# Reordering the column tiles of a projection so that each head pair's three tiles stand together

## The chip, the core and the metric

The kernel runs on one core of a Trainium2 chip. The time is the device time of one execution in microseconds (us). The engines are TensorE (PE; PEld is its weight loads), VectorE (DVE), ScalarE (ACT), GpSimd (POOL) and SyncE (SP), whose queue issues the DMAs here. Each engine works through its own queue in order; semaphores set by the other engines release what waits.

## What is computed

One layer of a mixed model over T = 2048 tokens of width 1024. The normalized input is multiplied by `w_in` (1024 x 3712, here 29 column tiles of 128), and the columns go to three branches, whose results go through one output projection:

```
h = rms_norm(x, pre_norm_g[i])
z = h @ w_in[i]
...
out_a = spatial_gating(u_a, v_a, ...) * silu(g_a)
out_b = conv_module(val_b, glu_b, ...) * silu(g_b)
out_c = rwkv7_mix(z[..., oc:og], ...) * silu(z[..., og:])
mix = concatenate([out_a, out_b, out_c]) @ w_out[i]
```

The third branch is a recurrence with eight heads of 64, worked on in four pairs. For each pair it needs a tile each of r, k and v. Ahead of the recurrence come a token shift, the decay (a small two-stage product with a sigmoid), the normalization of k within each head (`kk * rsqrt(max(sum(kk*kk), 1e-12))`) and the sum of r·k·r_k within each head, which multiplies v.

## The kernel before

The tokens are projected in two halves of 1024 (half 0 and half 1). A column tile of a half is `gemm` (L295 to L303): 48 matmuls of 128x512, three products of high and low parts in fp32r, eight steps of the inner dimension, two groups of tokens. Its result stands in one of two PSUM buffers `z` (`zps`), so that a tile can begin only when what reads the tile two places ahead of it is done. Half 0 projects all 29 tiles; half 1 projects the first 23 in this loop, and the last six (10, 11, 25 to 28) are spread out in `tail()`, beside the recurrence. Half 0 also splits each weight tile into parts (ScalarE L282, GpSimd L283) and stores them; half 1 reloads them.

The order of the tiles is the list `ORDER` (L349). `TG` gives each tile's place in it. The steps that use a tile are generators that yield due times made from `TG`; the scheduler takes these as priorities and sets each engine's order when the program is built. Nothing else is written out by hand for the projection.

What hangs on the tiles:

- Head pair p has the tiles 12+p (r), 16+p (k) and 20+p (v). `s_prep` prepares it: the small products of the decay (TensorE L469, L474; ScalarE L476, L478), a scan (VectorE L481), the token shift of each tile (ScalarE L329; VectorE L330, and L333 in half 1), the square of k (ScalarE L496), its high and low parts (`parts`: ScalarE L231, GpSimd or VectorE L232), the sums within heads on TensorE (`sums`, L240), the maximum (VectorE L501), the square root (ScalarE L503), four reciprocals (`recip`, VectorE L245), L505. After the v tile: VectorE L515 and L517; GpSimd L521, ScalarE L522, GpSimd L523; VectorE L525 and GpSimd L526; eight transposes of v (TensorE L537) with their copies (ScalarE L539); the product r·k (VectorE L546), its parts (L231, L232), the sums (TensorE L240), and L553 and L554.
- Tiles 4 and 5 need one ScalarE instruction (L592). Tiles 0 and 1 need a VectorE product (L595), small matmuls (TensorE L603) and two more VectorE steps (L607, L610).
- Tiles 8, 6, 9 and 7 feed a convolution over 31 taps: VectorE L452, 120 instructions over both halves. `s_pw` (L613) normalizes its result: sums (L240 with `onesm`), VectorE L625, ScalarE L630, sums again, ScalarE L637, the same `recip` (VectorE L245), VectorE L641, ScalarE L642.
- The recurrence begins, after the projection of half 1, with score matmuls at L819 and VectorE L824.

In the rows z, m and c are PSUM tiles, w weight tiles, h the normalized input, and L, mk, pg and inv work tiles.

Of the kernel before, what the change touches and what calls it, by code (L numbers as in the profile page):

```python
# [34 lines left out]
def hybrid_kernel(ctx, tc, x, x_t, w_in, vecs, wup, pw_w, sgu_wt, sgu_lnb, sgu_b,  # L35
# [310 lines left out]

    ORDER = [2, 8, 3, 6, 24, 9, 7, 12, 16, 13, 20, 17, 21, 4, 14, 0, 18, 22, 15, 19, 5, 23, 1, 10, 11, 25, 26, 27, 28]  # L349
    NG = len(ORDER)  # L350
    NT = 6
    LORD = [2, 3] + [ct for ct in ORDER if ct not in (2, 3)]
    TG = {ct: i for i, ct in enumerate(ORDER)}
    W, Z, H, X = {}, {}, {}, {}
# [38 lines left out]
    def s_gemm():  # L393
        for half in range(2):
# [5 lines left out]
            while n < (NG if half == 0 else NG - NT):  # L400
                two = half == 0 and n == NG - 2
                yield b0 + n
                cts = ORDER[n:n + 2] if two else ORDER[n:n + 1]
                for ct in cts:
# [282 lines left out]
    def tail():  # L687

        cts = ORDER[NG - NT:]
        for n, ct in enumerate(cts[:-2]):  # L690
# [655 lines left out]
```

## Time and profile before

| | before |
|---|---|
| three runs | 1484.35, 1481.45, 1483.39 us |
| median | 1483.39 us |
| the profiled execution | 1479.78 us |
| its span, first to last instruction | 1477.8 us |
| mean granted clock of TensorE | 0.977 |
| TensorE busy | 1389.8 us (94%) |
| VectorE busy | 997.8 us (68%) |
| ScalarE busy | 575.1 us (39%) |
| GpSimd busy | 351.4 us (24%) |

The busy shares are means over the whole span. Half 0 is projected from about 80 us to 430 us, half 1 from there to about 720 us, and the recurrence follows. In a timeline row, the first number is the start in us from the beginning of the span, the second the time from the first instruction's start to the last one's end, x the number of instructions; the bracket is the idle time ahead of it and what released it.

### The profile page before, as it was taken

The page shows a single profiled execution, that of the slowest core. Times are in us where ns is not written, and L with a number is a line of the kernel's source. Part 1 is how long each engine was busy: PE and PEld are TensorE (multiplying, and loading weights), DVE is VectorE, ACT ScalarE, POOL GpSimd, SP SyncE. Part 2 cuts the span into 40 slices and gives each one's busy share as a digit, 9 for nine tenths or more (in the row PEclk, how much of TensorE's full clock was granted, in tenths as well). Part 3 has the DMA queues.
Part 4 walks back from the last instruction along what each step waited for, and adds up shares of the span by engine and source line. Part 5 has one row for each costly group of instructions (what it writes and reads, how often), then busy time and mean ns, then how long its engine had stood idle before and what let it go on. Part 6 is the DMA issues. An engine that isn't in the chain of part 4 may idle for free.

```text
span 1477.8 us, 24438 instructions
## 1 busy us (share of the span) xinstructions
PE 1389.8 (94%) x9701; PEld 1108.8 (75%) x9701; DVE 997.8 (68%) x1963; ACT 575.1 (39%) x900; POOL 351.4 (24%) x324
## 2 busy tenths in 40 slices
PE   7999999999999999899898888989888999999998
PEld 6876777786798787678676767767766777888887
DVE  6599993674537999567767587687687654555553
ACT  6343344556322344454433444534434443212121
POOL 5443454542401023133211211211212100111110
PEclk9999999999999999999999999999999999999999
DMA  8432466579435457646724732233231443323231
GB/s 325 154 132 87 133 200 202 182 260 317 174 112 168 169 179 211 208 138 190 233 86 174 227 115 88 73 116 100 73 113 61 144 132 128 133 103 129 101 131 43
DMA packets 158311, 223.29 MB, mean 151 GB/s; under 512 B 58236, under 2 KB 108149, under 8 KB 158198
## 3 DMA queue, kind: packets, MB, share of 16 engines
q1 hardware_dynamic: 158066, 221.68, 45.6%
q8 instruction: 76, 1.25, 0.4%
q14 instruction: 37, 0.30, 0.1%
q10 hardware_dynamic: 132, 0.06, 0.0%
HBM read 132.58 MB, written 89.13 MB: 150 GB/s over the span
## 4 chain that ended last, share of the span: by engine, by line
PE 65%; DVE 24%; ACT 4%; issue 3%; DMA 2%; POOL 1%; DVEq 0%; ACTq 0%; POOLq 0%; SPq 0%
PE z L300 27%; PE z L1160 12%; PE z L1047 8%; DVE inv L452 7%; PE c L1137 3%; DVE inv L872 3%; PE z L312 2%; DVE inv L877 2%; PE m L819 2%; DVE mk L245 2%; PE m L240 1%; DVE L L975 1%; PE m L1116 1%; POOL L L268 1%; PE c L960 1%
## 5 line engine op out<-in xcount | busy, mean ns | idle before, releaser
L300 PE MATMUL z<-h,w 128*128 128x512 f32 x2592 | 636.1, 400 | 7.0 <-ACT zl L336 3.3
L300 PEld LDWEIGHTS z<-h,w 128*128 128x128 f32 x2592 | 486.8, 190 | 128.0 <-issue 7.1
L1047 PE MATMUL z<-h,w 128*128 128x512 f32 x768 | 211.4, 420 | 0.7 <-DVE w L1034 0.7
L452 DVE SCALAR_TENSOR_TENSOR inv<-inv,vc,inv 128x1024 f32<-128x1024 f32 x120 | 191.0, 1610 | 1.6
L1047 PEld LDWEIGHTS z<-h,w 128*128 128x128 f32 x768 | 143.8, 197 | 32.5 <-DVE w L1034 1.1
L283 POOL TENSOR_TENSOR w<-w,w 128x1024 fp32r<-128x1024 f32 x26 | 74.2, 2853 | 123.0 <-PE z L300 95.5
L1160 PE MATMUL z<-L,w 128*128 128x512 f32 (+1 forms) x384 | 96.4, 394 | 0.0
L1160 PE MATMUL z<-h,w 128*128 128x512 f32 (+1 forms) x384 | 93.3, 391 | 0.8 <-DVE inv L1143 0.8
L1144 ACT ACTIVATE inv<-inv 128x512 f32<-128x512 f32 (+1 forms) x33 | 20.4, 619 | 182.3 <-DVE inv L1143 182.3
L872 DVE TENSOR_TENSOR inv<-inv,inv 128x48 f32<-128x48 f32 (+23 forms) x464 | 87.5, 222 | 2.4
L1104 POOL TENSOR_TENSOR inv<-inv,pg 128x1024 f32<-128x1024 f32 x16 | 38.3, 2395 | 208.6 <-DMA inv<-mx_s 122.7
L877 DVE TENSOR_TENSOR inv<-inv,inv 128x48 f32<-128x48 f32 (+23 forms) x464 | 84.3, 218 | 1.2
L1160 PEld LDWEIGHTS z<-h,w 128*128 128x128 f32 x384 | 71.3, 188 | 17.3 <-DVE inv L1143 1.2
L1143 DVE TENSOR_TENSOR inv<-z,L 128x512 f32<-128x512 f32 (+1 forms) x32 | 21.9, 683 | 89.7 <-PE z L1160 89.7
L1160 PEld LDWEIGHTS z<-L,w 128*128 128x128 f32 x384 | 70.5, 188 | 15.5
L977 POOL TENSOR_TENSOR ri<-ri,pc 128x256 f32<-128x256 f32 x31 | 21.5, 695 | 240.3 <-DVE L L975 162.5
L245 DVE RECIPROCAL mk<-mk 128x256 f32<-128x256 f32 x40 | 65.8, 1709 | 18.1 <-ACT mk L503 9.3
L824 DVE TENSOR_TENSOR mk<-m,mask 128x512 f32<-128x512 f32 x58 | 37.6, 686 | 45.9 <-PE m L819 41.4
L819 PE MATMUL m<-L,L 64*128 64x128 f32 x464 | 44.9, 303 | 17.6 <-DVE inv L872 15.2
L828 ACT COPY inv<-mk 32x128 f32<-32x128 f32 x128 | 37.9, 296 | 55.3 <-DVE mk L824 52.4
L819 PEld LDWEIGHTS m<-L,L 64*128 64x128 f32 x464 | 37.2, 201 | 24.8 <-issue 20.0
L312 PE MATMUL z<-w,h 128*128 128x256 f32 x384 | 52.7, 293 | 0.9 <-ACT h L262 0.9
(246 smaller groups left out, 2019.9 us busy)
## 6 DMA issues: line engine op xcount, KB each, us to landing
w_s<-w SPq DMA_DIRECT2D x58, 512.0 KB, 3.3
w<-w_s SPq DMA_DIRECT2D x58, 512.0 KB, 5.2
w<-in_w_in_dram SPq DMA_DIRECT2D x26, 512.0 KB, 3.7
L<-in_x_dram SPq DMA_DIRECT2D x16, 512.0 KB, 7.9
ar_s<-L SPq DMA_DIRECT2D x16, 512.0 KB, 5.4
wo_s<-w SPq DMA_DIRECT2D x16, 512.0 KB, 3.4
L<-ar_s SPq DMA_DIRECT2D x32, 256.0 KB, 3.2
L<-bk_s SPq DMA_DIRECT2D x32, 256.0 KB, 4.1
```

The lines of the kernel that those rows point to most:

```text
L245: nc.vector.reciprocal(t[:, g * 256:(g + 1) * 256], t[:, g * 256:(g + 1) * 256])
L283: nc.gpsimd.tensor_tensor(out=ws[1], in0=wr, in1=ws[0], op=ALU.subtract)
L300: nc.tensor.matmul(z[:, g * 512:(g + 1) * 512], lhsT=ws[a][:, k * 128:(k + 1) * 128], rhs=h[:, b, k, :], start=(n == 0), stop=(n == 23))
L312: nc.tensor.matmul(z[:, i * 256:(i + 1) * 256], lhsT=h[:, b, k, i * 128:(i + 1) * 128], rhs=ws[k // 4][a][:, (k % 4) * 256:(k % 4 + 1) * 2 ...
L452: nc.vector.scalar_tensor_tensor(out=ac, in0=y[:, i:i + HT], scalar=col(V_CW + 2 * i + ct), in1=ac, op0=ALU.mult, op1=ALU.add)
L819: nc.tensor.matmul(sp[par][:, p, :], lhsT=bk[lo:lo + 64, p, :], rhs=ar[lo:lo + 64, p, :], start=True, stop=True)
L872: nc.vector.tensor_tensor(out=tmp[:, o:o + n, :m], in0=tl[:, lo:hi, m:m + 1].to_broadcast([128, n, m]), in1=ml[:, m, :m].unsqueeze(1).to_b ...
L877: nc.vector.tensor_tensor(out=tl[:, lo:hi, :m], in0=tl[:, lo:hi, :m], in1=tmp[:, o:o + n, :m], op=ALU.add)
L1047: nc.tensor.matmul(mx[:, nh * 512:(nh + 1) * 512], lhsT=oT[a][:, k, :], rhs=wo[k // 4][:, b, k % 4, nh * 512:(nh + 1) * 512], start=(k == ...
L1104: nc.gpsimd.tensor_tensor(out=x2, in0=x2, in1=pg[0], op=ALU.mult)
L1137: nc.tensor.matmul(pp, lhsT=pT[:, a, k, :], rhs=gw[8 + k][b][:, nh * 512:(nh + 1) * 512], start=(n == 0), stop=(n == 5))
L1160: nc.tensor.matmul(z, lhsT=xT[a][:, k, :], rhs=gw[k][b][:, sl], start=(k == 0 and n == 0), stop=(k == 7 and n == 2))
```

## The change

Only the list `ORDER` is changed.

```diff
-    ORDER = [2, 8, 3, 6, 24, 9, 7, 12, 16, 13, 20, 17, 21, 4, 14, 0, 18, 22, 15, 19, 5, 23, 1, 10, 11, 25, 26, 27, 28]
+    ORDER = [2, 8, 3, 6, 24, 9, 7, 12, 16, 20, 4, 0, 13, 17, 21, 5, 14, 18, 22, 1, 15, 19, 23, 10, 11, 25, 26, 27, 28]
```

The first nine tiles stay, and so do the last six. Between them, each pair's r, k and v now stand in a row. Pair 0 (12, 16, 20) is followed by 4 and 0, pair 1 (13, 17, 21) by 5, pair 2 (14, 18, 22) by 1, and pair 3 (15, 19, 23) by tile 10. The order holds for both halves.

In the order of TensorE's instructions, half 0, the sum of pair 0's r·k (m_1356 and m_1360, L240 on `ones64`) stands in z_1569, the product of tile 14:

```order
L300 MATMUL z_1569<-h_224,w_1346 128x512
L300 MATMUL z_1569<-h_224,w_1345 128x512 x2
L300 MATMUL z_1569<-h_224,w_1346 128x512
L240 MATMUL m_1356<-mk_1352,ones_83 128x512
L300 MATMUL z_1569<-h_224,w_1345 128x512
L240 MATMUL m_1360<-mk_1352,ones_83 128x512
L300 MATMUL z_1569<-h_224,w_1345 128x512
```

Now that sum (m_1245 and m_1249) stands in z_1367, the product of tile 13:

```order
L300 MATMUL z_1367<-h_289,w_1139 128x512
L300 MATMUL z_1367<-h_289,w_1138 128x512
L240 MATMUL m_1245<-mk_1241,ones_83 128x512
L240 MATMUL m_1249<-mk_1241,ones_83 128x512
L300 MATMUL z_1367<-h_289,w_1138 128x512
L469 MATMUL c_1321<-mk_766,ri_122 128x512
L474 MATMUL c_1321<-mk_766,yc_123 128x512
```

It has moved two tiles ahead, and short matmuls of pair 1 (L469, L474) stand just behind it.

VectorE's order at the same place, from pair 0's L515 to its L546, before:

```order
L515 SCALAR_TENSOR_TENSOR L_1234<-mk_1048,L_896 128x8x64
L515 SCALAR_TENSOR_TENSOR L_1238<-mk_1048,L_896 128x8x64
L517 TENSOR_TENSOR L_1238<-L_979,L_896 128x8x64
L452 SCALAR_TENSOR_TENSOR inv_894<-inv_890,vc,inv_894 128x1024 x2
L525 TENSOR_TENSOR mk_1048<-mk_1048,L_916 128x1024
L452 SCALAR_TENSOR_TENSOR inv_894<-inv_890,vc,inv_894 128x1024
L330 SCALAR_TENSOR_TENSOR L_1296<-z_1247,vc,L_1296 128x1023
L452 SCALAR_TENSOR_TENSOR inv_894<-inv_890,vc,inv_894 128x1024
L546 SCALAR_TENSOR_TENSOR L_979<-L_979,vc,L_1044 128x1024
```

and now:

```order
L515 SCALAR_TENSOR_TENSOR L_1144<-mk_1048,L_896 128x8x64
L515 SCALAR_TENSOR_TENSOR L_1148<-mk_1048,L_896 128x8x64
L517 TENSOR_TENSOR L_1148<-L_979,L_896 128x8x64
L452 SCALAR_TENSOR_TENSOR inv_894<-inv_890,vc,inv_894 128x1024 x2
L525 TENSOR_TENSOR mk_1048<-mk_1048,L_916 128x1024
L452 SCALAR_TENSOR_TENSOR inv_894<-inv_890,vc,inv_894 128x1024
L595 TENSOR_TENSOR mk_1207<-z_1257,mk_1207 128x1024
L452 SCALAR_TENSOR_TENSOR inv_894<-inv_890,vc,inv_894 128x1024
L546 SCALAR_TENSOR_TENSOR L_979<-L_979,vc,L_1044 128x1024
```

L330 of the next pair's k tile (L_1296) has left this stretch, and L595 of tile 0 has come in.

At the end of half 1's projection TensorE's order before is, from the last matmul of tile 10 (z_4922) over the transposes of pair 3 and the sum of its r·k (m_4852, m_4856) to the first scores:

```order
L300 MATMUL z_4922<-h_2839,w_4649 128x512
L537 MATMUL m_4833<-ident,L_4724 128x128 x4
L537 MATMUL m_4839<-ident,L_4724 128x128 x4
L240 MATMUL m_4852<-mk_4848,ones_83 128x512
L240 MATMUL m_4856<-mk_4848,ones_83 128x512
L240 MATMUL m_4852<-mk_4849,ones_83 128x512
L240 MATMUL m_4856<-mk_4849,ones_83 128x512
L603 MATMUL m_4863<-yc_124,mk_133 64x128 x8
L603 MATMUL m_4873<-yc_124,mk_134 64x128 x8
L819 MATMUL m_4971<-L_4889,L_4890 128x128
```

Now it is this, where m_4875 and m_4879 are pair 3's r·k sum:

```order
L300 MATMUL z_4922<-h_2839,w_4650 128x512
L300 MATMUL z_4922<-h_2839,w_4649 128x512
L537 MATMUL m_4856<-ident,L_4834 128x128 x4
L537 MATMUL m_4862<-ident,L_4834 128x128 x4
L240 MATMUL m_4875<-mk_4871,ones_83 128x512
L240 MATMUL m_4879<-mk_4871,ones_83 128x512
L240 MATMUL m_4875<-mk_4872,ones_83 128x512
L240 MATMUL m_4879<-mk_4872,ones_83 128x512
L819 MATMUL m_4971<-L_4889,L_4890 128x128
```

L603 of tile 1 has gone from this place. The second half of pair 3's key sums, m_4738, which stood nearly two tiles ahead of z_4922 before (as m_4582), is now in its first half:

```order
L300 MATMUL z_4922<-h_2814,w_4650 128x512
L300 MATMUL z_4922<-h_2814,w_4649 128x512 x2
L240 MATMUL m_4738<-mk_4730,ones_83 128x512
L240 MATMUL m_4738<-mk_4731,ones_83 128x512
L300 MATMUL z_4922<-h_2814,w_4650 128x512
L300 MATMUL z_4922<-h_2814,w_4649 128x512 x2
```

VectorE's order there, from pair 3's L501 to its L546, where mk_4740 is the norm of the convolution, before:

```order
L501 TENSOR_SCALAR mk_4572<-m_4578 128x512
L501 TENSOR_SCALAR mk_4572<-m_4582 128x512
L232 TENSOR_TENSOR mk_4654<-inv_3223,mk_4653 128x1024
L245 RECIPROCAL mk_4572<-mk_4572 128x256 x4
L232 TENSOR_TENSOR mk_4658<-inv_3421,mk_4657 128x1024
L505 SCALAR_TENSOR_TENSOR mk_4572<-L_4568,vc,mk_4572 128x1024
L517 TENSOR_TENSOR L_4757<-L_4473,L_4383 128x8x64
L515 SCALAR_TENSOR_TENSOR L_4757<-mk_4572,L_4383 128x8x64
L515 SCALAR_TENSOR_TENSOR L_4761<-mk_4572,L_4383 128x8x64
L517 TENSOR_TENSOR L_4761<-L_4473,L_4383 128x8x64
L330 SCALAR_TENSOR_TENSOR L_4724<-z_4675,vc,L_4724 128x1023
L333 SCALAR_TENSOR_TENSOR L_4724<-zl,vc,L_4724 128x1
```

with mk_4740 later, behind L546:

```order
L525 TENSOR_TENSOR mk_4572<-mk_4572,L_4403 128x1024
L232 TENSOR_TENSOR mk_4731<-mk_4728,mk_4730 128x1024
L546 SCALAR_TENSOR_TENSOR L_4473<-L_4473,vc,L_4568 128x1024
L595 TENSOR_TENSOR mk_4647<-z_4768,mk_4647 128x1024
L232 TENSOR_TENSOR mk_4737<-mk_4734,mk_4736 128x1024
L245 RECIPROCAL mk_4740<-mk_4740 128x256 x4
L641 TENSOR_TENSOR inv_3223<-inv_3223,mk_4740 128x1024
L641 TENSOR_TENSOR inv_3421<-inv_3421,mk_4740 128x1024
```

Now, from the second L501, with the norm of the convolution as mk_4760:

```order
L501 TENSOR_SCALAR mk_4728<-m_4738 128x512
L232 TENSOR_TENSOR mk_4757<-mk_4754,mk_4756 128x1024
L245 RECIPROCAL mk_4728<-mk_4728 128x256 x4
L245 RECIPROCAL mk_4760<-mk_4760 128x256 x4
L505 SCALAR_TENSOR_TENSOR mk_4728<-L_4724,vc,mk_4728 128x1024
L641 TENSOR_TENSOR inv_3223<-inv_3223,mk_4760 128x1024
L641 TENSOR_TENSOR inv_3421<-inv_3421,mk_4760 128x1024
L515 SCALAR_TENSOR_TENSOR L_4838<-mk_4728,L_4529 128x8x64
L515 SCALAR_TENSOR_TENSOR L_4842<-mk_4728,L_4529 128x8x64
L517 TENSOR_TENSOR L_4842<-L_4645,L_4529 128x8x64
L525 TENSOR_TENSOR mk_4728<-mk_4728,L_4549 128x1024
L546 SCALAR_TENSOR_TENSOR L_4645<-L_4645,vc,L_4724 128x1024
```

The two groups of four reciprocals stand next to each other, ahead of L515, and L641 stands between L505 and L515.

## Rows read from the trace of the kernel before

**Rows 1.** Busy time by stretch: us, engines in order, granted clock, DMA share, GB/s.

```profile
180.00:200.00 20.00, 14.05 (x47) 10.25 (x46) 19.93 (x14) 4.48 (x6) 10.28 (x4) 0.83 0.65 184
600.00:620.00 20.00, 15.73 (x82) 11.33 (x81) 8.20 (x11) 8.59 (x9) 2.36 (x1) 0.83 0.69 213
700.00:720.00 20.00, 15.77 (x76) 12.10 (x76) 16.44 (x11) 8.72 (x10) 5.25 (x4) 0.86 1.03 281
```

**Rows 2.** Timeline of TensorE, half 0: start, us, instructions, idle ahead and its releaser.

```profile
147.99 32.92 PE L300 MATMUL z<-h,w 128*128 128x512 f32 x141
184.25 0.73 PE L300 MATMUL z<-h,w 128*128 128x512 f32 x2 [3.33 <-ACT zl L336]
186.37 1.22 PE L240 MATMUL m<-mk,ones 128*128 128x512 f32 x2 [1.39 <-ACT mk L231]
...
200.11 1.26 PE L537 MATMUL m<-ident,L 128*128 128x128 f32 x8 [1.34 <-DVE mk L501]
```

**Rows 3.** Timeline of TensorE in the projection of half 1.

```profile
525.97 0.62 PE L240 MATMUL m<-mk,ones 128*128 128x512 f32 x2
...
563.04 0.72 PE L240 MATMUL m<-mk,ones 128*128 128x512 f32 x2 [1.58 <-POOL mk L232]
...
571.49 1.25 PE L537 MATMUL m<-ident,L 128*128 128x128 f32 x8 [1.46 <-DVE mk L501]
...
592.87 0.50 PE L469 MATMUL c<-mk,ri 128*128 128x512 f32 x1 [1.14 <-ACT L L476]
...
603.74 0.73 PE L300 MATMUL z<-h,w 128*128 128x512 f32 x2 [1.39 <-DVE L L330]
...
607.59 1.22 PE L240 MATMUL m<-mk,ones 128*128 128x512 f32 x2 [2.88 <-ACT mk L231]
```

**Rows 4.** Timeline of TensorE at the junction to the recurrence.

```profile
713.08 0.98 PE L240 MATMUL m<-mk,ones 128*128 128x512 f32 x2 [1.18 <-ACT mk L231]
715.52 1.22 PE L240 MATMUL m<-mk,ones 128*128 128x512 f32 x2 [1.45 <-POOL mk L232]
718.33 3.34 PE L603 MATMUL m<-yc,mk 128*64 128x128 f32 x32 [1.60 <-DVE L L553]
721.60 0.38 PE L819 MATMUL m<-L,L 64*128 64x128 f32 x1
```

**Rows 5.** Timeline of VectorE ahead of the junction.

```profile
658.38 3.52 DVE L546 SCALAR_TENSOR_TENSOR L<-L,vc,L 128x1024 f32<-128x1024 f32 x1 [2.53 <-POOL L L523]
...
674.58 1.38 DVE L501 TENSOR_SCALAR mk<-m 128x512 f32<-128x512 f32 x2 [4.51 <-PE m L240]
...
680.08 6.59 DVE L245 RECIPROCAL mk<-mk 128x256 f32<-128x256 f32 x4 [2.09 <-ACT mk L503]
...
689.45 1.29 DVE L515 SCALAR_TENSOR_TENSOR L<-mk,L 128x512 f32<-128x512 f32 x2
...
714.23 3.45 DVE L641 TENSOR_TENSOR inv<-inv,mk 128x1024 f32<-128x1024 f32 x2
```

**Rows 6.** Timeline of VectorE in the projection, half 0 and half 1.

```profile
144.87 2.31 DVE L481 TENSOR_TENSOR_SCAN L<-inv,L 128x1040 f32<-128x1040 f32 x1
...
182.74 1.27 DVE L330 SCALAR_TENSOR_TENSOR L<-z,vc,L 128x1023 f32<-128x1023 f32 x1
...
186.05 1.27 DVE L546 SCALAR_TENSOR_TENSOR L<-L,vc,L 128x1024 f32<-128x1024 f32 x1
...
557.35 3.42 DVE L546 SCALAR_TENSOR_TENSOR L<-L,vc,L 128x1024 f32<-128x1024 f32 x1
```

**Rows 7.** Timelines of GpSimd and ScalarE ahead of the junction.

```profile
658.42 2.40 POOL L526 TENSOR_TENSOR L<-L,L 128x1024 f32<-128x1024 f32 x1
...
690.88 2.73 POOL L521 TENSOR_TENSOR mk<-mk,mk 128x1024 f32<-128x1024 f32 x1 [19.92 <-issue]
694.97 2.41 POOL L523 TENSOR_TENSOR L<-L,mk 128x1024 f32<-128x1024 f32 x1 [1.36 <-ACT mk L522]
...
711.98 1.05 ACT L231 CAST mk<-L 128x1024 fp32r<-128x1024 f32 x1
```

## The prediction

> **What bounds the kernel now.** I read the granted clock by stretch first [rows 1], then TensorE's timeline through the projection of half 0 [rows 2], of half 1 [rows 3] and across the junction to the recurrence [rows 4], and then the engines that the waits there name [rows 5 to 7]. TensorE is busy 94% of the span, so in the projection each idle microsecond is a microsecond of the time. In [rows 2 to 4] the bracket on a row is TensorE's idle time ahead of it and who released it. Half 0 waits 3.33 + 1.39 + 1.34 = 6.06 us between 180 and 202 us; half 1 waits 1.58 + 1.46 + 1.14 + 1.39 + 2.88 = 8.45 us between 561 and 608; at the junction, after the last matmul of tile 10's projection and ahead of the recurrence's first scores, 1.18 + 1.45 + 1.60 = 4.23 us. A fourth wait near 141 us stands ahead of where the new order makes a difference, and I leave it out.
>
> With the waits comes a slower clock: the granted clock is 0.83 in 180–200 and in 600–620 and 0.86 in 700–720 [rows 1]. TensorE goes between full speed and half speed (2.4 and 1.2 GHz), so 0.83 over 20 us is 0.17 × 20 × 2 = 6.8 us at half speed, in which 3.4 us of full-speed work are lost. So the waits of half 0 cost 6.1 + 3.4 = 9.5 us, those of half 1 8.45 + 3.4 = 11.85 us.
>
> Most releasers are ScalarE's L231 or VectorE lines of head-pair preparation. Behind them stands VectorE, which works without a gap in these stretches: in 180–200 it is busy 19.93 of 20 us [rows 1], and its queue holds convolution taps (L452) between the preparation's steps.
>
> **What the change does.** No instruction is added or removed; the 29 tiles are multiplied in another order, and the scheduler places the steps that follow them. It changes three places; what I read from the order of the instructions is shown ahead of this part of the document.
>
> *Half 0, tiles 12 to 14.* One full-speed projection matmul is 32.92 / 141 = 0.2335 us [rows 2]. In the order after, from the last of pair 0's key sums (m_1058) to the sum of its r·k product (m_1245) TensorE has 128 projection matmuls, eight transposes (1.0, [rows 2]) and six small matmuls (0.2 each): 128 × 0.2335 + 2.2 = 32.1 us. Before, the same sums end at 148.0 and 201 projection matmuls stand between. So TensorE is at the new sum at 148.0 + 32.1 = 180.1. Its input is the product at L546, then the cast at L231. L546 starts at 186.05 before [rows 6]. Its VectorE queue after has the same fourteen L452 ahead of it from 139 us on, but one L481 (2.31) and two L330 (1.27 each, a little of it under the next instruction, so 1.2) fewer [rows 6], and one L595 (an operation of the same shape, 1.1) more: 186.05 − 3.6 = 182.5. With 1.27 for itself and 1.05 for L231 [rows 6, 7] the sum can start at about 185: a wait of 4.9 us, 6.3 if the taps ahead of L546 take 1.4 longer, say 5.5. A slow clock behind it costs what such a one costs before, 3.4 at most, say 3. Two small things are added: the short matmuls that stood between tile 16's and tile 13's no longer cover the buffer's release (0.9), and I allow 1.4 for a weight split on GpSimd at the end of the half. New cost 5.5 + 3 + 2.3 = 10.8, against 9.5: **+1.3 us**, between −4 and +4.
>
> *Half 1, the same five tiles.* From the key sums (end near 526.4, [rows 3]) the order after has 123 projection matmuls until the matmul L469 of c_3860, 28.7 + 2.2 us: TensorE is there at 557.3. That matmul waits for ScalarE's L478, which is queued behind L231, which waits for L546. L546 before ends at 557.35 + 3.42 = 560.8 [rows 6]; after, two L330 fewer stand ahead of it and the small ones cancel, so 558.5. With L231 (1.05) and L478 (some 0.7) it is 560.5 to 562: a wait of **4 us**, without room for a slow clock in my sum. Against 11.85 this is **−7.9 us**, between −11.85 (no wait) and −1 (7.5 with a slow clock, and 3.4 of the old waits again).
>
> *The junction.* Before, pair 3's key tile (19) is followed by tiles 5, 23 and 1 and then 10; its key sums end near 674.6 and the r·k sum stands at 713.08, with 138 projection matmuls between (32 us). After, tile 19 is followed by 23 and 10 alone; the second half of pair 3's key sums (m_4738) stands inside tile 10, eleven projection matmuls in, and the r·k sum (m_4875) behind its last one. Between the two TensorE has 35 projection matmuls, eight L240 and eight transposes: 35 × 0.2335 + 8 × 0.235 + 0.8 = 10.9 us. Behind m_4875 stand the first scores (L819) and with them everything else on TensorE.
>
> The chain from the one sum to the other runs on four engines, and VectorE's queue holds two more steps in it. From the start of L501: L501 twice 1.38; table load and square root on ScalarE 2.6 (the gap is 4.1 before, of which ScalarE spent part on casts); L245 four times 6.59 for pair 3; L245 four times another 6.59, since the reciprocals of the convolution's norm stand next in the queue [rows 5]; L505 1.2 (the shape of L546 at 186.05, [rows 6]); L641 twice 2.4, for the same reason (3.45 before, while GpSimd worked beside it); L515 twice 1.3; GpSimd's L521 2.9 with its start; L522 with its handing over 1.36 (the bracket of L523); L523 2.4 [rows 7]; L546 3.5, behind L526; L231 1.05. The sum is 33.3 us. TensorE waits 33.3 − 10.9 = 22.4 us, and 1.5 more for the low half of the product, as before (1.45, [rows 4]): 23.9 against 4.23, **+19.7 us**. Its ends: L546 at 1.27 instead of 3.5 and no wait for the low half, 16; 4.1 for the square root's gap and 3.45 for L641, 22.5. The slow clock at the junction I leave as it is; if its half-speed stretch falls into the idle time, up to 3.4 come back.
>
> L546 deserves its own line: on VectorE it takes 1.27 us at 186.05 [rows 6] but 3.52 at 658.38, started while GpSimd's L526 runs [rows 5, 7], and the queues bring the two together again after the change. The Trainium skill, "SBUF — State Buffer", section "Who interferes with whom", says that a VectorE instruction with two SBUF inputs contends with a GpSimd instruction that reads SBUF. By that rule 3.5 stands in the sum, and the row agrees; without it the sum would be 2.2 us less.
>
> **Sum.** +1.3 − 7.9 + 19.7 = +13.1 us. From the first scores on, TensorE's and VectorE's orders are the same as before, so the shift is carried to the end unchanged. The profiled execution took 1479.8 us (its span is 1477.8), 3.6 below the median of the runs, 1483.4: 1493 on its scale, **1496 us** on the median's.
>
> **Rivals.** *A, no wait is left in the two halves.* L546 of pair 0 is on time in both: in half 0 it would have to be 5.5 us earlier than counted, in half 1 4 us. VectorE's taps vary from 1.2 to several us each where GpSimd runs beside them, so that is not excluded. Then both halves give back 9.5 + 11.85 = 21.4 us, and with the junction at 19.7 the time is 1482, no change; with the junction at its low end (16, and up to 3.4 of slow clock gained) it is 1474 to 1478, **faster**. It decides from where the two halves give back more than the junction takes, that is 19.7. Against it: VectorE is busy all through these stretches and its work is only moved.
>
> *B, the waits of the halves only move.* VectorE's total work up to the junction is the same; if the new waits with their slow clock come to as much as the old ones, nothing is gained ahead of the junction and the time is 1483 + 20 = 1503, up to 1508 with the junction's high end. For it: the same full VectorE. Against it: L546 sits 2 to 4 us earlier in its queue.
>
> *C, the junction is covered*, because the chain's steps start earlier than the order suggests. The queue order of each engine is fixed, and m_4738 can't be earlier than its matmul, so the chain of 33 us can't begin earlier. Even without the reciprocals and L641 of the convolution (9 us) it is 24.3, and TensorE waits 13. With that the time is 1483 + 1.3 − 7.9 + 10.7 = 1487.
>
> **Chances and range.** My forecast 0.63, B 0.12, C 0.04: slower. A 0.21, of which 0.11 faster and 0.10 no change. A measurement of this kernel can tell some 0.2%, 3 us, from no change. So faster 0.11, no change 0.10, slower 0.79. The range is 1481 to 1507: it takes in most of A's no change, C, the forecast with the ends of its terms (+1 to +26 over 1483 taken together), and leaves out the faster part of A, and B's upper end.
>
> **What would show it.** Right: on TensorE one wait of about 22 us at an L240 released by ScalarE's L231 just ahead of the first L819, which starts some 13 us later than the 721.6 of before [rows 4]; on VectorE, ahead of it, two groups of L245 in a row; one wait of 4 to 6 us in each half near L546 of pair 0, in place of three and five. Wrong: a junction with less than 16 us of idle time; or waits in the halves that come to less than 3 us, or to as much as before; or a shift at the first scores that the tail doesn't carry to the end.

## The result: 1.6% slower, nearly twice the loss that was forecast

| | before | changed |
|---|---|---|
| median | 1483.3 us | 1506.8 us |
| runs | 1481.5 to 1484.4 | 1505.7 to 1507.4 |
| span of the profiled execution | 1477.8 us | 1505.7 us |
| mean granted clock | 0.977 | 0.968 |
| TensorE busy | 1389.8 us (94%) | 1391.0 us (92%) |

The ratio is 1.0163 (95% interval 1.0151 to 1.0176): 23.4 us on the medians, where 12.6 were forecast. The sign and the wait at the junction came as forecast. The time lies at the upper edge of the range (1507); measured by the ratio it is just over it.

The profile after, TensorE's timeline, which answers to [rows 2]. The columns are the start, the time taken, the instructions and the idle time ahead with its releaser:

```profile
141.58 0.72 PE L240 MATMUL m<-mk,ones 128*128 128x512 f32 x2 [1.62 <-ACT mk L231]
...
175.07 0.50 PE L469 MATMUL c<-pg,ri 128*128 128x512 f32 x1 [1.87 <-ACT L L476]
...
186.40 1.22 PE L240 MATMUL m<-mk,ones 128*128 128x512 f32 x2 [5.32 <-ACT mk L231]
...
200.04 1.97 PE L603 MATMUL m<-yc,mk 128*64 128x128 f32 x32 [1.96 <-DVE L L553]
...
376.17 6.25 PE L300 MATMUL z<-h,w 128*128 128x512 f32 x20 [8.74 <-ACT pg L653]
...
393.01 7.27 PE L300 MATMUL z<-h,w 128*128 128x512 f32 x24 [3.22 <-ACT pg L559]
```

Half 0 ends with two waits, the last two rows, 8.74 and 3.22 us, together 11.96. Before, the waits of over 0.9 us there were one of 1.19, also for L653, and one of 0.96 for L283. (L653 is ScalarE's first step on tiles 10 and 11, L559 its step on tiles 25 to 28; each reads a PSUM buffer `z`, and TensorE can't start the tile two places on before that.) In its middle, the rows above, is the wait that was forecast: 5.32 us at the sum behind L546 (forecast 4.9 to 6.3, taken 5.5).

The projection of half 1, for [rows 3], and the junction, for [rows 4]:

```profile
450.90 9.26 PE L300 MATMUL z<-h,w 128*128 128x512 f32 x39
...
573.54 2.84 PE L300 MATMUL z<-h,w 128*128 128x512 f32 x6 [2.43 <-DMA w<-w_s]
...
717.34 1.04 PE L537 MATMUL m<-ident,L 128*128 128x128 f32 x8
739.40 1.22 PE L240 MATMUL m<-mk,ones 128*128 128x512 f32 x2 [21.03 <-ACT mk L231]
741.89 1.22 PE L240 MATMUL m<-mk,ones 128*128 128x512 f32 x2 [1.27 <-POOL mk L232]
743.47 0.58 PE L819 MATMUL m<-L,L 64*128 64x128 f32 x1 [0.36 <-DVE L L553]
```

Half 1's middle has one wait of more than half a microsecond left, 2.43 us for a reloaded weight tile, against 8.45 before. At the junction TensorE waits 21.03 + 1.27 + 0.36 = 22.66 us, against 4.23.

The account of the profiled execution, at points that both kernels have. Tile 6, the fourth tile of half 1, begins at 450.90, before at 439.05: half 0 is 11.85 us longer (at half 1's first tile the shift is 12.0 already). The first scores begin at 743.47, before at 721.60, so half 1 is 10.0 longer. The span is 27.9 us longer, so 6.0 more are lost behind the first scores. This execution of before was one of its shorter ones, which is why its difference is larger than that of the medians.

### The profile page after: what moved, and what is told of

The parts are those of the page before. It is cut to its first block, busy times and chain, and to the rows that moved or that the text cites. A ratio compares the mean times of both kernels' runs of the same rounds, so it can differ in the third digit from the quotient of the medians.

```text
span 1505.7 us, 24436 instructions
## 1 busy us (share of the span) xinstructions
PE 1391.0 (92%) x9701; PEld 1111.4 (74%) x9701; DVE 985.5 (65%) x1963; ACT 573.6 (38%) x897; POOL 349.2 (23%) x324
## 4 chain that ended last, share of the span: by engine, by line
PE 64%; DVE 23%; DMA 4%; ACT 4%; issue 3%; POOL 1%; SPq 1%; DVEq 0%; ACTq 0%; POOLq 0%
PE z L300 27%; PE z L1160 12%; PE z L1047 8%; DVE inv L452 6%; PE c L1137 3%; PE z L312 2%; PE m L819 2%; DVE mk L245 2%; DVE inv L872 2%; DVE inv L877 2%; DVE L L975 1%; PE m L1116 1%; PE m L240 1%; DMA w<-in_gate_w_dram 1%; PE c L960 1%
## 5 line engine op out<-in xcount | busy, mean ns | idle before, releaser
L452 DVE SCALAR_TENSOR_TENSOR inv<-inv,vc,inv 128x1024 f32<-128x1024 f32 x120 | 185.5, 1565 | 1.8
L283 POOL TENSOR_TENSOR w<-w,w 128x1024 fp32r<-128x1024 f32 x26 | 72.2, 2777 | 124.5 <-PE z L300 86.7
L330 DVE SCALAR_TENSOR_TENSOR L<-z,vc,L 128x1023 f32<-128x1023 f32 x24 | 30.7, 1278 | 42.3 <-ACT L L329 42.3
```

Source lines behind the costliest of these rows:

```text
L283: nc.gpsimd.tensor_tensor(out=ws[1], in0=wr, in1=ws[0], op=ALU.subtract)
L452: nc.vector.scalar_tensor_tensor(out=ac, in0=y[:, i:i + HT], scalar=col(V_CW + 2 * i + ct), in1=ac, op0=ALU.mult, op1=ALU.add)
```

## Half by half

**The new order in one half alone.** The list is split, and each half takes its own; the second kernel has the two lists exchanged.

```diff
-    ORDER = [...]
+    ORDERS = [new order, order of before]
...
-                cts = ORDER[n:n + 2] if two else ORDER[n:n + 1]
+                cts = ORDERS[half][n:n + 2] if two else ORDERS[half][n:n + 1]
```

> The new order in half 0 alone, the old one in half 1. Theory (the two ends of the halves, each on its own): TensorE's idle time at the end of half 0 is that of the changed kernel, 8.7 + 3.2 us ahead of the readers of L653 and L559, the junction is that of before (some 4 us idle), and the time is 12 us over before, some 1495. Rival (the wait at the end of half 0 is taken back by half 1, whose stages wait for other engines anyway): within 3 us of before.

Measured: 1493.1 us, ratio 1.0065 (1.0042 to 1.0087). TensorE's timeline:

```profile
376.09 6.44 PE L300 MATMUL z<-h,w 128*128 128x512 f32 x20 [8.85 <-ACT pg L653]
...
393.08 7.17 PE L300 MATMUL z<-h,w 128*128 128x512 f32 x23 [3.17 <-ACT pg L559]
...
725.69 0.99 PE L240 MATMUL m<-mk,ones 128*128 128x512 f32 x2 [1.18 <-ACT mk L231]
```

The two waits are those of the changed kernel (8.85 and 3.17), and the junction is that of before, 1.18 at its first wait. Half 1 takes nothing back.

> The old order in half 0, the new one in half 1. Theory: 22 us idle at the junction against 4, a slow clock in the first scores (2 us), 7 us fewer in the middle of half 1: some 12 us over before, 1495; no wait over 2 us at the end of half 0. Rival (the junction is late because half 0 left the engines behind): the junction's idle time falls below 15 us and the time is within 5 us of before.

Measured: 1493.3 us, ratio 1.0061 (1.0044 to 1.0079), 9.4 over before.

TensorE's timeline again:

```profile
369.54 4.94 PE L300 MATMUL z<-h,w 128*128 128x512 f32 x20 [0.63 <-ACT pg L653]
...
394.90 5.39 PE L300 MATMUL z<-h,w 128*128 128x512 f32 x22 [1.35 <-POOL w L283]
...
726.41 1.22 PE L240 MATMUL m<-mk,ones 128*128 128x512 f32 x2 [21.03 <-ACT mk L231]
```

The end of half 0 waits 0.63 and 1.35 us; the junction has its 21.03 in full. So half 0 costs 9.2 us, half 1 9.4, and each comes without the other. Their sum, 18.7, is somewhat less than the 23.4 of both; the two intervals are wide enough for 2 us of that each.

## Which part of the order

**Pair 3 alone.** Pairs 0 to 2 stand as before, and pair 3 is put last.

```diff
-    ORDER = [..., 14, 0, 18, 22, 15, 19, 5, 23, 1, 10, ...]
+    ORDER = [..., 14, 0, 18, 22, 5, 1, 15, 19, 23, 10, ...]
```

> Only pair 3 is regrouped and put last (tiles 5, 1, 15, 19, 23 in place of 15, 19, 5, 23, 1); pairs 0 to 2 stand as before. Theory (all of the loss is pair 3's place): the junction's 22 us and the end of half 0's 12 us are both there, and the middles keep the waits of before: 25 to 30 us over before, 1508 to 1513. Rival (the grouping of the other pairs makes the loss): less than 10 us over before.

Measured: 1514.0 us, ratio 1.0188 on runs that scatter (1508 to 1517; interval 1.0159 to 1.0217), 28 to 30 over before.

TensorE's timeline:

```profile
376.60 6.28 PE L300 MATMUL z<-h,w 128*128 128x512 f32 x20 [7.45 <-ACT pg L653]
...
394.61 5.78 PE L300 MATMUL z<-h,w 128*128 128x512 f32 x13 [4.36 <-ACT pg L559]
...
749.24 1.22 PE L240 MATMUL m<-mk,ones 128*128 128x512 f32 x2 [19.55 <-ACT mk L231]
```

The loss comes at the same two places, which these three rows show (and, as in the changed kernel, 5 us more behind the first scores), and the waits of the middle of half 1 are back (1.55, 1.47, 1.13, 1.33 and 2.89 us).

**Pairs 0 to 2 alone**, pair 3 with the tiles around it as before.

```diff
-    ORDER = [..., 12, 16, 13, 20, 17, 21, 4, 14, 0, 18, 22, 15, 19, 5, 23, 1, 10, ...]
+    ORDER = [..., 12, 16, 20, 4, 0, 13, 17, 21, 14, 18, 22, 15, 19, 5, 23, 1, 10, ...]
```

> Pairs 0 to 2 are regrouped, pair 3 with the tiles around it stands as before (15, 19, 5, 23, 1). Theory: the junction idles 4 to 6 us and the end of half 0 some 2 us as before, the middle of half 1 gives 5 to 8 us back and half 0's middle 0 to 3: 1473 to 1479, faster than before. Rival (the waits of the middles only move to the later pairs, since VectorE is full there): within 3 us of before; or slower by over 5 if the grouping itself makes the loss at the end of half 0.

Measured: 1474.6 us, ratio 0.9942 (0.9927 to 0.9958): 9 us faster than before. One of its nine executions, the profiled one, took 1482.5; the others 1472.7 to 1476.2. So it was run again:

> The kernel with pairs 0 to 2 regrouped once more, since its profiled execution was 8 us longer than its other runs. Theory (the stalls of the middles vary with how VectorE and GpSimd meet, and that one execution had more slow clock): 1472 to 1477 in nearly all runs, with a mean granted clock of 0.98. Rival (the gain was chance): within 3 us of before.

Measured: 1475.5 us, ratio 0.9954 (0.994 to 0.9968), and a profiled execution with a span of 1473.4. Its TensorE timeline at the end of half 0, in half 1 and at the junction:

```profile
395.97 4.25 PE L300 MATMUL z<-h,w 128*128 128x512 f32 x11 [2.93 <-POOL w L283]
...
564.60 1.66 PE L300 MATMUL z<-h,w 128*128 128x512 f32 x6 [2.01 <-DMA w<-w_s]
...
707.10 0.98 PE L240 MATMUL m<-mk,ones 128*128 128x512 f32 x2 [1.18 <-ACT mk L231]
...
712.35 3.04 PE L603 MATMUL m<-yc,mk 128*64 128x128 f32 x26 [2.09 <-DVE L L553]
```

In half 1 there is one wait of 2.01 us where before has five; the junction is that of [rows 4] but for half a microsecond. Regrouping the pairs is a gain. The loss is pair 3's place.

**One tile behind pair 3.** The changed kernel with tile 1 moved to the end.

```diff
-    ORDER = [..., 5, 14, 18, 22, 1, 15, 19, 23, 10, ...]
+    ORDER = [..., 5, 14, 18, 22, 15, 19, 23, 1, 10, ...]
```

> The changed kernel with one tile moved: 1 stands behind pair 3 (14, 18, 22, 15, 19, 23, 1) instead of ahead of it, in both halves. In the order of the instructions 137 projection matmuls now stand between pair 3's last key sum and its r·k sum (35 in the changed kernel), and pair 3's last ScalarE step of half 0 (L554) stands behind all eight squares of half 1's input (L210). Theory (pair 3's place makes the whole loss): the junction idles 4 to 6 us, the end of half 0 under 5, and the time is that of the kernel with pairs 0 to 2 regrouped, 1472 to 1479. Rival (the regrouping of pairs 0 to 2 costs as well, or the loss is in the number of light tiles between the pairs): over 1490.

Measured: 1489.1 us, ratio 1.0051 (1.0039 to 1.0063). Neither number came: it is 18 us better than the changed kernel, but 14 short of what I expected.

TensorE's timeline, end of half 0 and junction:

```profile
366.55 1.98 PE L661 MATMUL c<-inv,jk 128*128 128x512 f32 x4 [0.73 <-ACT inv L642]
...
377.97 7.46 PE L300 MATMUL z<-h,w 128*128 128x512 f32 x20 [5.01 <-ACT pg L653]
...
716.76 0.73 PE L240 MATMUL m<-mk,onesm 128*128 128x512 f32 x2 [2.61 <-DVE mk L232]
...
723.22 1.22 PE L240 MATMUL m<-mk,ones 128*128 128x512 f32 x2 [1.16 <-POOL mk L232]
```

The junction's waits are small, these two and four under 0.8 us. At the end of half 0, 5.01 us are waited for L653 again. ScalarE's row of it, and SyncE's:

```profile
376.89 1.02 ACT L653 ACTIVATE pg<-z 128x1024 f32<-128x1024 f32 x1 [8.43 <-DMA ab_s<-pg]
```

```profile
365.56 3.04 SPq L223 DMA_DIRECT2D L<-in_x_t_dram  x1
...
369.68 1.23 SPq L666 DMA_DIRECT2D ab_s<-pg  x1
```

Here ScalarE has no square right ahead of L653. It waits 8.43 us for the store of the first result of L653, of which there is one buffer (`pg`). That store (L666) is issued at 369.68, behind an input load (L223, 3.04 us in issuing) and two other stores, and lands 7.1 us later. So a late store alone is enough to make L653 late.

This is half of the shortfall. Against the kernel with pairs 0 to 2 regrouped, TensorE is 6.8 us later at tile 6 of half 1 and loses 6.0 more up to the first scores; of these, 1.4 are waits, and the rest goes with a slower clock (0.91, 0.95 and 0.79 in 560–580, 700–720 and 720–740, against 1.00, 0.83 and 1.00).

## The end of half 0

The order of ScalarE in the changed kernel, where `z_2458` is tile 11, the L210 are squares of half 1's input, and L554 is pair 3's last step:

```
L210 ACTIVATE L_2559,ssq_2558<-L_2559 128x1024
L554 ACTIVATE L_2331<-L_2331,vc 128x1024
L210 ACTIVATE L_2562,ssq_2558<-L_2562 128x1024
L653 ACT_TABLE_LOAD
L653 ACTIVATE pg_2507<-z_2458 128x1024
```

Before, all eight L210 and L554 stand ahead of this table load, but the first input loads were issued at 314.28; in the changed kernel they are issued at 344.17. SyncE's rows, first of before, then of the changed kernel, and ScalarE's of the changed kernel:

```profile
314.28 1.92 SPq L209 DMA_DIRECT2D L<-in_x_dram  x2
...
357.86 0.56 SPq L666 DMA_DIRECT2D ab_s<-pg  x1
```

```profile
344.17 2.37 SPq L209 DMA_DIRECT2D L<-in_x_dram  x3
...
366.74 0.38 SPq L209 DMA_DIRECT2D L<-in_x_dram  x1
367.22 0.75 SPq L666 DMA_DIRECT2D ab_s<-pg  x1
```

```profile
366.92 1.06 ACT L210 ACTIVATE L<-L 128x1024 f32<-128x1024 f32 x1 [4.19 <-DMA L<-in_x_dram]
...
368.55 1.15 ACT L554 ACTIVATE L<-L,vc 128x1024 f32<-128x1024 f32 x1 [0.48 <-DVE L L553]
372.45 1.06 ACT L210 ACTIVATE L<-L 128x1024 f32<-128x1024 f32 x1 [2.75 <-DMA L<-in_x_dram]
...
373.80 1.28 ACT L653 ACT_TABLE_LOAD   x1 [0.20 <-DMA ab_s<-pg]
375.09 1.02 ACT L653 ACTIVATE pg<-z 128x1024 f32<-128x1024 f32 x1
```

The squares at 366.92 and 372.45 wait 4.19 and 2.75 us for their inputs; the load of the second was issued at 366.74. L653, which frees tile 11's PSUM buffer, stands right behind them, and TensorE waits for that until 376.17. But L653 also writes `pg`, and so waits for the store of tile 10's result. Its data is ready at 360.1, but the store is issued at 367.22, behind an input load and other DMAs (before: ready at 357.1, issued at 357.86); it lands 6.5 us later, and by the bracket at 373.80 it is the last to end, 0.20 us behind the square. The wait of 3.22 us ends in the same way: L559 writes `pg` too, and waits for the store of tile 11's result. So L653 is late by two ways at once, the squares in ScalarE's queue and the store in the DMA queue, and the late input loads crowd both. The edit moves these loads: it makes half 1's input due 2.5 tiles earlier, which tells them from pair 3's work, but not the one way from the other:

```diff
-            b0 = half * (NG - 3.5)
+            b0 = half * (NG - 6.0)
```

> The new order in half 0 alone, and the input of half 1 (its DMAs L209, L223 and the squares L210 on ScalarE) due 2.5 tiles earlier. In ScalarE's order the second reader L653 then stands behind all eight L210, which come earlier, and ahead of it stands nothing that was just loaded. Theory (the end of half 0 waits because L653 stands in ScalarE's queue behind squares whose input is loaded late, after pair 3's preparation): the wait of 8.8 us at L653 falls under 3, the one at L559 may stay, and the time is 1483 to 1488. Rival (TensorE waits for pair 3's preparation or for the weights, whatever ScalarE's order): 8 us and more stay, 1492.

Measured: 1482.3 us, ratio 0.9999 (0.9989 to 1.0008), against 1493.1 without the edit.

TensorE's timeline, and ScalarE's row of L653:

```profile
370.60 29.78 PE L300 MATMUL z<-h,w 128*128 128x512 f32 x127 [1.60 <-ACT pg L653]
```

```profile
369.52 1.02 ACT L653 ACTIVATE pg<-z 128x1024 f32<-128x1024 f32 x1 [1.57 <-DMA ab_s<-pg]
```

The wait of 8.85 is 1.60, the one of 3.17 is gone: after 370.60 TensorE runs 127 projection matmuls without a wait. The first result's store is issued at 366.39, hardly earlier than without the edit (367.04), but lands 3.1 us later instead of 6.6, while the DMA engines' mean busy share in 360–380 is 0.47 instead of 1.01. So half 0's loss was not the time of pair 3's work, but the loads that came late with it. The same edit on the whole changed kernel:

> The changed kernel whole (both halves in the new order) with the input of half 1 due 2.5 tiles earlier. Theory (half 0's end and the junction are two separate losses): the wait of 8.7 us at the second L653 and the one of 3.2 at L559 go, the junction keeps its 21 us of idle time, and the time falls by 9 to 12 us from 1506.8 to 1495 to 1498. Rival (what is saved at the end of half 0 is waited for later in half 1): over 1502.

Measured: 1494.3 us, ratio 1.0080 (1.0068 to 1.0092), 12.5 us under the changed kernel.

TensorE's timeline:

```profile
369.58 30.64 PE L300 MATMUL z<-h,w 128*128 128x512 f32 x124 [1.90 <-ACT pg L653]
...
727.31 1.22 PE L240 MATMUL m<-mk,ones 128*128 128x512 f32 x2 [21.03 <-ACT mk L231]
```

What is left over before, 11.7 us, is the junction's loss less what the middle of half 1 gives (by this trace 9.0 us from tile 6 to the first scores), and what is lost behind the first scores (5.1).

That pair 3's place moves the loads, the runs show: the first L209 is issued at 343.8 to 344.6 in the three kernels that have pair 3 right ahead of tile 10 in half 0, at 327.4 with tile 1 between them, and at 314.3 to 319.0 where pair 3 stands as before (all with the input due as before). In the changed kernel it follows pair 3's store of v (L541, 342.99) in the queue, without a wait of its own. That the order puts it there because pair 3 holds the work tiles (`L`) that it would be loaded into is likely, but not shown: no kernel with more such tiles was run.

## The junction

VectorE's timeline in the changed kernel, which answers to [rows 5]:

```profile
706.51 0.68 DVE L501 TENSOR_SCALAR mk<-m 128x512 f32<-128x512 f32 x1
...
710.67 13.03 DVE L245 RECIPROCAL mk<-mk 128x256 f32<-128x256 f32 x8 [1.33 <-ACT mk L503]
723.62 1.18 DVE L505 SCALAR_TENSOR_TENSOR mk<-L,vc,mk 128x1024 f32<-128x1024 f32 x1
724.73 2.35 DVE L641 TENSOR_TENSOR inv<-inv,mk 128x1024 f32<-128x1024 f32 x2
...
734.81 3.46 DVE L546 SCALAR_TENSOR_TENSOR L<-L,vc,L 128x1024 f32<-128x1024 f32 x1 [2.47 <-POOL L L523]
```

The eight reciprocals stand in a row, 13.03 us. From the start of the first L501 (706.51) to the end of L546 are 31.8 us, and to the sum at 739.40 32.9 (forecast 33.3). L546 takes 3.46 us, beside GpSimd's L526 (734.85 to 737.19), as [rows 5, 7] had it, where the L546 at 184.00 in half 0 takes 1.27. The Trainium skill, "SBUF — State Buffer", section "Who interferes with whom", says that a VectorE instruction with two SBUF inputs contends with a GpSimd instruction that reads SBUF; this trace agrees with it.

Whether VectorE's queue sets the wait is shown by taking the reciprocals of the convolution's norm out of it, in half 1, with the old order in half 0:

```diff
-        recip(rb)
+        recip(rb) if half == 0 else None
```

> The new order in half 1 alone, and the four reciprocals of the convolution's norm left out in half 1 (the branch of the convolution is scaled wrongly there), so that they don't stand in VectorE's queue between pair 3's reciprocals and L505. TensorE has the same 35 projection matmuls between the two sums. Theory (the junction is VectorE's queue, step by step): the 21 us of idle time become 14.5, and the time is 6 to 7 us under that of the new order in half 1 (1493): 1486 to 1487. Rival (the chain over ScalarE and GpSimd ends later than VectorE's and sets the wait): 19 to 21 us idle and the same time.

TensorE's row of the wait, and VectorE's rows of the chain:

```profile
723.76 1.22 PE L240 MATMUL m<-mk,ones 128*128 128x512 f32 x2 [14.74 <-ACT mk L231]
```

```profile
701.32 6.59 DVE L245 RECIPROCAL mk<-mk 128x256 f32<-128x256 f32 x4 [1.33 <-ACT mk L503]
707.83 2.29 DVE L641 TENSOR_TENSOR inv<-inv,mk 128x1024 f32<-128x1024 f32 x2
710.03 1.28 DVE L505 SCALAR_TENSOR_TENSOR mk<-L,vc,mk 128x1024 f32<-128x1024 f32 x1
```

L641 follows the first four reciprocals at once, and the 21.03 us are 14.74: 6.29 less for 6.5 us of VectorE's work. The rival is out. The time is 1490.1 us (ratio 1.0050, 1.0031 to 1.0068), 3.2 under the 1493.3 with the reciprocals, where 6 to 7 were expected; four runs between 1485.8 and 1493.0 don't tell whether the rest is lost behind the junction or is scatter. In the profiled execution, the longest of the four, tile 6 to the first scores is 4.8 us shorter than with the reciprocals, but half 0, whose order is the same, is 2.2 longer, and 2.0 more are lost behind the first scores.

## A version that is faster than both

If the halves add, the best is a half 0 without its end's wait and a half 1 with pairs 0 to 2 regrouped. Three kernels, with the edits shown above (per-half lists, the regrouped front, the earlier input):

> The order of before in half 0; in half 1 pairs 0 to 2 regrouped and pair 3 as before (15, 19, 5, 23, 1). Theory (the gain of the kernel with pairs 0 to 2 regrouped is made in the middle of half 1 alone, where TensorE's stretch from the first projection of half 1 to the first scores was 9 us shorter, while its half 0 was 3 us longer): 1471 to 1475, faster than before and not slower than with both halves regrouped (1475). Rival (half 0's regrouping had a share in the gain): 1478 to 1481.

Measured: 1474.6 us, ratio 0.9945 (0.9933 to 0.9957). The gain is made in half 1 alone.

> The new order in half 0 with the input of half 1 due 2.5 tiles earlier, and pairs 0 to 2 regrouped in half 1 with pair 3 as before. Theory (the halves add): half 0 as in the run with the earlier input (no change against before), half 1 9 us shorter: 1472 to 1476. Rival (the earlier input takes buffers from half 1's first tiles): over 1480.

Measured: 1473.4 us, ratio 0.9932 (0.992 to 0.9945). The halves add.

> Pairs 0 to 2 regrouped in both halves, pair 3 as before, and the input of half 1 due 2.5 tiles earlier. Theory (the second L653 doesn't stand behind late squares in this order, and the 2.9 us that are left there wait for GpSimd's weight split L283): no change from 1475, within 3 us. Rival (the crowd on the DMA queue at the end of half 0 is what the earlier input thins out): 3 us or more faster, under 1472.

Measured: 1471.6 us, ratio 0.9925 (0.9912 to 0.9939), 11 us faster than before. The 2.93 us at the end of half 0 (L283) are gone, with no wait over half a microsecond there. The gain over the kernel without the earlier input (1474.6 and 1475.5 in two other groups of runs) is about the 3 us that decided between the two theories, so that the rival is likely but not settled; this kernel and the two above can't be told apart by these runs. Of all that were run it has the lowest median.

## Why the forecast was short

*Half 0, middle: right.* Forecast +1.3, of which 1.4 is for the weight split at the end of the half, so −0.1 for the middle. The waits between 120 and 202 us come to 13.5 us (the four rows above, 10.8, and three under 1 us) against 9.4. The wait near 141, which I had left out, is among them and did change (3.37 before, 1.62 now). The slow clock in this place varies: in 140–160 it is 0.83 before, 1.00 in the changed kernel, and 0.83 again in the kernel with the same order of half 0 alone. A better measure is the time at which TensorE comes to its wait for L653, with the same work done: 367.43 now (376.17 − 8.74) against 367.87. So the middle is 0.4 us shorter. The wait at the sum behind L546, 5.32 us, is the one forecast. L546 started at 184.00, 1.5 us later than counted, since the taps ahead of it took longer, inside what the range allowed.

*Half 0, end: the step that failed.* I allowed 1.4 us for a weight split on GpSimd. From the wait for L653 on, the end of half 0 costs 12.3 us more than before (11.85 + 0.4): the waits there are 11.96 us against 2.15, and behind them the clock is 0.83 in 360–380 and 0.91 in 380–400, where before has 1.00. I had followed pair 3's delay on the engines up to the recurrence in half 1, but in half 0 only looked for who works for TensorE, not for what a reader of PSUM stands behind in its own queue, nor for when the buffer that it writes comes free. Pair 3's place moved the loads of half 1's input by 30 us; L653 stood behind their squares, and the store that frees its buffer stood in the crowd of the loads themselves. Moving the loads took the wait away (8.85 to 1.60), and with it 12.5 us of the changed kernel's time. Which of the two ways would have held L653 by itself is not separated.

*Half 1, middle: right in size, wrong in place.* Forecast −7.9 with a wait of 4 us at L469. That wait isn't there; one of 2.43 for weights is, with half a stretch of slow clock (0.91 in 560–580): 8.45 + 3.4 against 2.43 + 1.8, −7.6. That the size came out is luck: the wait that I had derived from L546 did not come, and the one that came was not in my sum.

*The junction: right.* Forecast 23.9 us idle, measured 22.66; the steps in its sum are the rows above, and the reciprocals' share was shown by leaving them out.

*Behind the first scores: not in the sum.* I had carried the shift to the end unchanged. It grows by 6.0 us in this execution, which is one of the signs of being wrong that I had named. The granted clock by stretch, changed kernel, for the last of [rows 1]:

```profile
720.00:740.00 20.00, 0.60 (x2) 0.50 (x2) 13.57 (x11) 5.01 (x5) 7.90 (x4) 0.51 0.89 271
740.00:760.00 20.00, 18.37 (x105) 12.15 (x104) 8.73 (x13) 6.90 (x18) 8.29 (x19) 0.81 0.87 254
```

In 740–760 the clock is 0.81, where before has 0.97 in its 720–740: the first scores run at half speed (0.58 us for the first against 0.38 in [rows 4]; the next ones start every 0.21 us instead of every 0.11). The shift is 21.9 at the first score and 23.9 at the seventeenth, with six matmuls of 128x512 between. That is 2.0 of the 6. I had taken the slow clock of the junction as the same in both kernels; after 22 us of idle time it lasts into the work that follows. The rest comes in steps of 1 to 2 us later in the recurrence, without a change in its order, and what makes it is open. It is not scatter alone: in the four executions with a wait of 19 to 21 us at the junction, 761.3 to 762.2 us lie behind the first scores; in before and the two with its half 1, 755.6 to 756.2.

Added up for this execution: −0.4 + 12.3 + 10.0 (the junction 18.4, so −8.4 for the middle of half 1) + 6.0 = 27.9 us, against the forecast's +13.1. Two terms make the difference: the end of half 0, and what comes behind the first scores.

Of the rivals, A is half right on half 1 (it gave 7.6 of its 11.85) and wrong on half 0's middle, which gave nothing. B is right on half 0's middle, where the waits only moved, and wrong on half 1; that the time lies among its numbers (1503 to 1508) is chance, since the end of half 0 is not in them. C was not seen.

## What to carry to other kernels

Before a group of tiles is moved later, follow not only its own chain to the next stage, but also the queues and buffers that others wait for behind it: here half of the loss came with an input load for the next half, which uses nothing that the group computes. The last group of a stage needs work behind it that covers its whole chain; what reads like a regular pattern ("each group followed by a light tile") is worth most at the end, where this order had tile 10 alone for a chain of 33 us. And when a change mixes a gain and a loss, split it by place and by half: the part that gains (pairs 0 to 2) was worth 7.5 to 9 us by itself.

## What the runs showed of the hardware

After a wait of 22 us TensorE's clock was still at half speed (1.2 GHz) when work came back: the granted clock is 0.51 in 720–740 and 0.81 in 740–760, and the first score took 0.58 us instead of 0.38. In 740–760 the clock's loss is at most 0.19 × 20 = 3.8 us, of which 2.0 fell behind the first scores; after waits of 1 to 5 us, a stretch at 0.83 cost 3.4. In this one case the long wait cost hardly more clock than the short ones.

The time of a VectorE reciprocal of 128x256 elements is 13.03 / 8 = 1.63 us, more than a product of four times as many elements (L641, 2.35 / 2 = 1.18 us), and two groups of four next to each other are the largest item of the junction's chain.

A store of 512 KB took 6.5 and 6.6 us from issue to landing where the DMA engines' mean busy share was 1.05 and 1.01, and 3.1 us where it was 0.47 (L666 in the changed kernel, with the new order in half 0 alone, and there with the earlier input; the shares are those of 360–380).
